# Shifting the start addresses of matmul operands within 512 bytes, stage by stage

## The chip, the cores and the metric

The kernel runs on one NeuronCore of a Trainium2 chip. The metric is the device time of one execution in microseconds, from the first to the last instruction and what lies around them. TensorE (PE) multiplies: each matmul loads a stationary operand of up to 128x128 (LDWEIGHTS, shown as PEld) and then streams a moving operand of up to 512 columns past it; both come from the on-chip memory SBUF, the sum goes to PSUM. VectorE (DVE), ScalarE (ACT) and GpSimd (POOL) work elementwise; transfers are issued from the queues of SyncE (SP), ScalarE and GpSimd.

## The reference

One layer of a streaming encoder on 4096 prompt frames and 32 sample frames, 1024 channels, all in float32:

```python
h = rmsnorm(x, norm_g)
u, v, z_a, xb, z_b = split(h @ w_in)                 # w_in 1024 x 5120
a = u * chunk_mlp(layernorm(v), w_spatial) * silu(z_a)    # 8 heads, 128x128 mixing inside chunks
b = pool_mix(xb) * silu(z_b)                         # trailing means over 2/4/8/16, then 256x256 per group
y = rmsnorm(x + concat(a, b) @ w_out, final_g)       # w_out 2048 x 1024
```

The pooling buffers of both streams and the normalised v rows of the sample frames are outputs as well.

## The kernel before

Each float32 factor is split into a high part (rounded to float32r, the type that TensorE multiplies in one pass) and a low part, and a product of two factors is taken as three matmuls: high x high, high x low, low x high. On top of that each pair of tiles is multiplied by a scheme with 7 products instead of 8 (`NQ = 7`, index `q`), whose operands are sums and differences of quarter blocks. One product `q` is thus 4 slices of the contraction (`k`) times 3 terms, 12 matmuls, all added up in one PSUM bank (lines 188 to 194, `product`); a set of 7 is 84 matmuls of 512 columns.

The work is in stages:

- The first pass (up to about 397 us of the span) normalises and transposes the tokens, makes the operands of all token blocks, and multiplies them with the v columns of `w_in`. Here the moving operand is a weight tile in a `slot` buffer, the stationary one an `op` tile of tokens. 16 pairs of tiles, 16 x 84 = 1344 matmuls.
- Token blocks 0 to 3 (to 1704 us), of 1024 tokens each: 8 gate sets and 8 pool sets per block. The 7 moving operands of a block, one per `q`, stay in the 7 `slot` buffers for the whole block; the stationary operands are weight tiles `wop`, made just ahead by ScalarE (the high part, line 119) and VectorE (the low part, line 81) out of `raw` tiles and of sums of them in `sum` tiles (line 115). Blocks 0 to 2 take 16 x 84 = 1344 matmuls of 512 columns each. Block 3 has the 32 sample frames with it, 528 columns, as 2 x 264: 2688 matmuls. Gate sets also do eight small matmuls for the mixing inside a chunk (line 998). Results pass through `t` tiles and go to DRAM as `abT`.
- The output projection in two halves, `z = 0` and `z = 1` (to the end): the moving operands are weights in the slots again, the stationary ones token tiles in `wop` buffers, read back from `abT`. 16 pairs and 1344 matmuls per half (lines 712 to 714). Sums are made in `y` tiles (line 724).

`product` names the operands: `stationary(s, k)` is 128 floats wide, so it starts at a multiple of 512 bytes within its tile of 1024 floats; `moving(m, k)` starts at a multiple of 512 bytes within the slot in all stages but block 3, where a slice is 528 floats (2112 bytes) long.

The order of the instructions is that in which the code issues them, apart from what the framework's scheduler moves for priority; `prepare` (line 1109 on) makes the stationary operands five products ahead of their use (`LEAD = 5`). When a stage ends, the slot of product `q` is filled anew behind the last product that read it: `Tokens.load` (line 922) and `load_out_weights` (line 632). The last two sets of a stage, and the first two of the next, are interleaved (`lagged`, line 181), so that there are products to do meanwhile. A first filling of the slots for block 0 is in `load_first` (line 589).

SBUF is laid out by pools, each behind the one before; `pool` opens one. The pools `raw_p`, `op_p` (tile `wop`), `sum_p`, and later `t_p`, `cn_p` or `y_p` follow the slots from the left; `WT`, `bias` and the `spare` and `vt` tiles stand at the right end. In the built program the slot buffers begin at byte 18432 (36 x 512) and are 16896 bytes (33 x 512) apart, the first `raw` buffer begins at 136704 (267 x 512), the first `wop` buffer at 161280 (315 x 512), `sum` at 189952 (371 x 512), and `y` and the first `t` at 196096 (383 x 512); `t` tiles are 2176 bytes (4 x 512 + 128), so they follow each other at 0, 128, 256 and 384 past a multiple of 512.

Of the kernel before, what the change touches and what calls it, by code (L numbers as in the profile page):

```python
# [8 lines left out]
F32 = mybir.dt.float32  # L9
F32R = mybir.dt.float32r  # L10
# [5 lines left out]
P = 128  # L16
D = 1024
# [8 lines left out]
NB = 4  # L26
# [3 lines left out]
WIDE = HALF + EXT  # L30
TOT = SEQ + DEC
NQ = 7
WARM = 14


@with_exitstack
def stream_step(ctx: ExitStack, tc, x_prompt, x_sample, state_pool, norm_g, w_in, ln_v_g, ln_v_b,
# [18 lines left out]
    slots = ctx.enter_context(tc.tile_pool(name="slots", bufs=NQ))  # L56
# [45 lines left out]
        return y, guess + 3 * [lambda: stt(t, y, y, m, ALU.mult, ALU.mult),  # L102
                               lambda: stt(y, t, 1.5, y, ALU.add, ALU.mult)]

    def slot():
        return slots.tile([P, 2 * 4 * WIDE], F32R, tag="slot", name="slot")


    behind = []
# [95 lines left out]
    def pool(name, bufs, stack=ctx, **kw):  # L205
        return stack.enter_context(tc.tile_pool(name=name, bufs=bufs, reuse_waits="tile", **kw))
# [4 lines left out]
    with ExitStack() as ph:  # L211
# [23 lines left out]
        def tr_tile():  # L235
            return ps_tr.tile([P, 512], F32, tag="tr", name="tr")

        g_bc = g_p.tile([P, D], F32, name="g_bc")
        first_ops = {}
# [9 lines left out]
        warm = tr_tile()  # L249
        for _ in range(WARM):  # L250
            tc.keep_in_program_order(nc.tensor.transpose(warm[:, :P], ident, ident))
# [10 lines left out]


        wv = [slot()[:, :8 * HALF].rearrange("p (h k n) -> p h k n", h=2, n=HALF) for _ in range(NQ)]

        v_raws = {}
# [87 lines left out]
        class Past:  # L354


            def load(self):
                self.st = half(), half()
                for z in range(2):
                    nc.gpsimd.memset(self.st[z][:HALO], 0.0)  # L360
                    nc.sync.dma_start(self.st[z][1:HALO], state_pool[0, 0, :, z * 512:(z + 1) * 512])
# [226 lines left out]

        def load_first(q):

            first_ops[q] = t = slot()
            dst = t[:, :8 * HALF].rearrange("p (h j x) -> p h j x", h=2, j=4)
            src = xops[0].rearrange("j p (q h x) -> q h p j x", q=NQ, h=2)
            n = 2 if q < NQ - 1 else 4
            for h in range(2):
                nc.sync.dma_start(dst[:, h, :n].bitcast(F32), src[q, h, :, :n])
            if n == 4:
                return
            nc.vector.tensor_copy(dst[:, :, pa.j], pa.ops[q])
            nc.scalar.copy(dst[:, :, pb.j], pb.ops[q])  # L600
# [4 lines left out]
        for n, (pair, q) in enumerate(lagged(pa, pb)):  # L605
            for step in {0: steps[:2], 1: steps[2:3], 2: steps[3:4], 4: steps[4:5], 6: steps[5:6], 7: steps[6:]}.get(n, []):
                step()
            if n == 1:
                norms([], [(v, P) for v in pairs[-3].v])
                pairs[-3].store()  # L610
            pair.product(q)
            if pair is pb:
                load_first(q)


    raw_p = pool("raw_p", 6)
    op_p = pool("wop_p", 7)
    sum_p = pool("sum_p", 3)
    ps_acc = pool("ps_acc2", 6, space=bass.MemoryType.PSUM)
# [10 lines left out]
    w_slots = {}  # L630

    def load_out_weights(z, q):
        w_slots[z, q] = t = slot()[:, :4 * D].rearrange("p (k h n) -> p k h n", k=4, h=2)
        nc.sync.dma_start(t.bitcast(F32), wops[z, q].rearrange("p k (h n) -> p k h n", h=2))

    class OutWeights:
# [227 lines left out]
    with ExitStack() as ph:  # L864
# [50 lines left out]
        class Tokens:  # L915
# [4 lines left out]
                self.groups = [(0, HALF)] if not self.last else [(0, WIDE // 2), (WIDE // 2, WIDE // 2)]  # L920

            def load(self, q):
                t = slot()
                self.ops[q] = t
                if self.last:
                    nc.sync.dma_start(t.bitcast(F32), xops_l[q].rearrange("p x t -> p (x t)"))
                    return
                src = xops[self.b].rearrange("j p (q h x) -> q h p j x", q=NQ, h=2)
                for h in range(2):
                    dst = t[:, h * 4 * HALF:(h + 1) * 4 * HALF].rearrange("p (j x) -> p j x", j=4)  # L930
                    nc.sync.dma_start(dst.bitcast(F32), src[q, h])
# [214 lines left out]
        for n in range(n_sets):  # L1146
# [9 lines left out]
            for s, q in order:  # L1156
                at += 1
                prepare(at + LEAD)
                while later:
                    (later.pop(0) or (lambda: None))()  # L1160
                for c, c0, w in cs[id(s)]:
                    s.product(c, q, c0, w)
                if n == 0 and q == 0:
                    behind.append(s)
                if s is g[-1] and groups[n + 1][0].stage != s.stage:
                    if n + 1 < n_sets:
                        groups[n + 1][0].tok.load(q)
                    else:
                        if q == 3:
                            groups[n_sets][1].begin([raw_tile(), raw_tile()], True)  # L1170
                        load_out_weights(0, q)
                if n == 0 and s is g[-1] and q in (3, 5):
                    next(constants, None)
                if s.kind == "gate" and q in (2, 4):
                    if q == 2:
                        s.t1 = []
                    s.t1.append(s.spatial(len(s.t1)))
                if s.kind == "gate" and q == 6 and s.tok.last:
                    s.spatial_sample()
                if q == NQ - 1:  # L1180
                    later.append(s.finish_gate() if s.kind == "gate" else s.finish_pool())
# [4 lines left out]
    with ExitStack() as ph:  # L1186
# [56 lines left out]
        for n in range(n_sets, len(groups)):  # L1243
# [6 lines left out]
            for m, (s, q) in enumerate(order):  # L1250
                at += 1
                prepare(at + LEAD)
                if m == 0 and n in samples:
                    samples[n].load()
                k = n - n_sets - 4
                if k == KT and m == 2:
                    sample_rows()
                if 0 <= k < KT and m in (0, 2):
                    state_load(k) if m == 0 else state_split()
                s.multiply(q)  # L1260
                if n == n_sets and s is g[0] and q == NQ - 1:
                    s.finish()
                if m == 2 and ended:
                    for x in ended:
                        x.finish()
                if s is g[-1] and n + 1 < len(groups) and groups[n + 1][0].stage != s.stage:
                    load_out_weights(1, q)
                if 0 <= k < KT and m == 6:
                    state_rows(k)
# [34 lines left out]
```

## Time and profile before

| | |
|---|---|
| median of 2 runs | 2346.66 us (2346.46 to 2346.87) |
| profiled execution, span | 2345.9 us |
| TensorE busy | 2328.8 us, 99% |
| weight loads (PEld) busy | 1981.3 us, 84%, beside the matmuls |
| VectorE / ScalarE / GpSimd busy | 1790.2 (76%) / 896.4 (38%) / 215.1 us (9%) |
| granted TensorE clock, mean | 0.999 |
| matmuls of line 193, 512 columns | 4032 with `wop`, 1344 with `op` |
| matmuls of line 193, 264 columns | 2688 |

How to read the lines: a row of a group gives the code line, the engine, the operation, the tiles written and read (out<-in), the count and the mean duration. The duration of a matmul covers its way through the array and overlaps the next one; what counts for the end is the pitch, the time from one start to the next. It is read off the chain of waits, which merges an unbroken run of like matmuls into one piece (start, length, count), or off the starts in a timeline.

### The profile page before, as it was taken

Reading aid. Unit: us, or ns where it says so; the run is one execution under the profiler, and the core shown is the slowest. Engines: PE = TensorE matmul, PEld = TensorE weight load, DVE = VectorE, ACT = ScalarE, POOL = GpSimd, SP = SyncE. Lnnn points to the kernel's source line nnn. Section 1 sums busy time; section 2 is a strip of 40 time slices with the busy share of each in tenths; the row PEclk is TensorE's granted clock in tenths of the full one; section 3 lists DMA queues with packets and bytes.
Section 4 is the critical chain, followed back from the end, with each engine's and each line's share of the span. In section 5 each row is a group of like instructions: output and inputs, shape, how many; then the busy total and the mean of one; then the engine's idle time right before and its main releaser. Section 6 shows DMA issues by size and latency. Waiting matters only on the chain.

```text
span 2345.9 us, 32604 instructions
## 1 busy us (share of the span) xinstructions
PE 2328.8 (99%) x11936; PEld 1981.3 (84%) x11936; DVE 1790.2 (76%) x3318; ACT 896.4 (38%) x1603; POOL 215.1 (9%) x398
## 2 busy tenths in 40 slices
PE   8999999999999999999999999999999999999998
PEld 7878888888888888888888899999987878888877
DVE  7877786866787767877668876668777778688887
ACT  6545544433433333433334333334322333233333
POOL 1010000100021000111000110102200000000000
PEclk9999999999999999999999999999999999999999
DMA  8879977432448334483334472335587776955542
GB/s 309 316 241 279 275 255 245 142 104 89 149 144 296 99 100 134 135 300 122 108 108 148 177 262 87 101 100 164 223 294 265 252 257 232 360 171 169 159 137 90
DMA packets 325145, 445.69 MB, mean 190 GB/s; under 512 B 19324, under 2 KB 248444, under 8 KB 322296
## 3 DMA queue, kind: packets, MB, share of 16 engines
q1 hardware_dynamic: 273384, 355.05, 45.9%
q0 software_dynamic: 22288, 73.48, 8.3%
q10 hardware_dynamic: 29312, 15.08, 2.4%
q8 instruction: 94, 1.54, 0.3%
q14 instruction: 67, 0.55, 0.1%
HBM read 273.88 MB, written 169.66 MB: 189 GB/s over the span
## 4 chain that ended last, share of the span: by engine, by line
PE 95%; DMA 2%; DVE 2%; issue 0%; ACT 0%; SPq 0%; ACTq 0%; DVEq 0%
PE acc L193 66%; PE acc L712 8%; PE acc L713 8%; PE acc L714 8%; PE sp L998 2%; PE tr L473 1%; DMA wops<-raw 1%; DMA vt<-in_w_in_dram 1%; PE acc L261 0%; DMA op<-in_w_in_dram 0%; PE more L844 0%; PE more L843 0%; DVE wop L81 0%; DVE y L724 0%; PE acc L202 0%
## 5 line engine op out<-in xcount | busy, mean ns | idle before, releaser
L193 PE MATMUL acc<-slot,wop 128*128 128x512 f32 (+1 forms) x6720 | 1260.9, 348 | 1.0 <-DVE wop L81 1.0
L193 PEld LDWEIGHTS acc<-slot,wop 128*128 128x128 f32 x6720 | 1081.1, 188 | 156.5 <-DVE wop L81 1.4
L81 DVE TENSOR_TENSOR wop<-raw,wop 128x512 fp32r<-128x512 f32 (+1 forms) x510 | 353.4, 695 | 133.0 <-ACT wop L119 121.7
L119 ACT CAST wop<-raw 128x512 fp32r<-128x512 f32 x340 | 210.5, 622 | 384.4 <-PE acc L193 266.9
L712 PE MATMUL acc<-slot,wop 128*128 128x512 f32 x892 | 347.2, 389 | 1.5 <-DVE y L724 1.5
L713 PE MATMUL acc<-slot,wop 128*128 128x512 f32 x892 | 347.1, 389 | 0.0
L714 PE MATMUL acc<-slot,wop 128*128 128x512 f32 x892 | 347.0, 389 | 0.0
L193 PE MATMUL acc<-slot,op 128*128 128x512 f32 x1344 | 323.8, 395 | 0.3 <-ACT vt L167 0.2
L193 PEld LDWEIGHTS acc<-slot,op 128*128 128x128 f32 x1344 | 247.6, 188 | 51.9 <-ACT vt L167 0.7
L165 DVE TENSOR_TENSOR t<-acc,t 128x512 f32<-128x512 f32 (+1 forms) x320 | 186.7, 584 | 120.0 <-ACT t L174 65.5
L724 DVE TENSOR_TENSOR y<-acc,y 128x512 f32<-128x512 f32 x235 | 159.3, 687 | 72.6 <-PE acc L714 72.2
L712 PEld LDWEIGHTS acc<-slot,wop 128*128 128x128 f32 x892 | 167.4, 188 | 37.8 <-ACT wop L677 2.3
L714 PEld LDWEIGHTS acc<-slot,wop 128*128 128x128 f32 x892 | 167.4, 188 | 34.8
L713 PEld LDWEIGHTS acc<-slot,wop 128*128 128x128 f32 x892 | 167.4, 188 | 34.7
L677 ACT CAST wop<-raw 128x512 fp32r<-128x512 f32 x160 | 98.7, 622 | 175.2 <-PE acc L714 164.9
L81 DVE TENSOR_TENSOR wop<-sum,wop 128x512 fp32r<-128x512 f32 x200 | 136.9, 685 | 25.7 <-ACT wop L119 24.9
L1017 POOL DMA_DIRECT2D abT<-t x128 | 69.2, 541 | 843.2 <-DVE t L1029 622.7
L119 ACT CAST wop<-sum 128x512 fp32r<-128x512 f32 x136 | 84.5, 622 | 96.9 <-PE acc L193 72.0
L1040 DVE TENSOR_TENSOR t<-t 128x527 f32<-128x527 f32 (+3 forms) x160 | 111.1, 698 | 0.6
L677 ACT CAST wop<-sum 128x512 fp32r<-128x512 f32 x64 | 39.7, 622 | 119.5 <-PE acc L714 96.3
L174 ACT COPY t<-acc 128x512 f32<-128x512 f32 (+1 forms) x80 | 40.2, 504 | 107.1 <-PE acc L193 105.4
L115 DVE TENSOR_TENSOR sum<-raw 128x512 f32<-128x512 f32 x68 | 46.8, 688 | 44.7 <-DMA raw<-in_w_in_dram 44.1
(236 smaller groups left out, 1955.0 us busy)
## 6 DMA issues: line engine op xcount, KB each, us to landing
raw<-in_w_in_dram SPq DMA_DIRECT2D x102, 512.0 KB, 4.3
xops<-op SPq DMA_DIRECT2D x72, 512.0 KB, 6.1
abT<-t POOLq DMA_DIRECT2D x128, 256.0 KB, 3.8
raw<-abT SPq DMA_DIRECT2D x64, 512.0 KB, 5.0
slot<-xops SPq DMA_DIRECT2D x30, 1024.0 KB, 9.6
slot<-wops SPq DMA_DIRECT2D x14, 2048.0 KB, 9.7
xt<-in_x_prompt_dram SPq DMA_DIRECT2D x32, 512.0 KB, 5.0
raw<-v_all SPq DMA_DIRECT2D x32, 512.0 KB, 3.3
```

The lines of the kernel that those rows point to most:

```text
L81: return nc.vector.tensor_tensor(out, src, hi.bitcast(F32), ALU.subtract)
L119: pair = nc.scalar.copy(hi, src), lo_part(lo, src, hi)
L165: add = lambda o, x, y: nc.vector.tensor_tensor(o, x, y, ALU.add)
L193: mm(acc, stationary(s, k), moving(m, k), start=fresh and n == 0, stop=n == len(terms) - 1, skip_group_check=True)
L677: nc.scalar.copy(t[:, 0], src)
L712: mm(acc, x[:, 0, k, :], w[:, k, 0, c], start=fresh and k == 0, stop=False, skip_group_check=True)
L713: mm(acc, x[:, 0, k, :], w[:, k, 1, c], start=False, stop=False, skip_group_check=True)
L714: mm(acc, x[:, 1, k, :], w[:, k, 0, c], start=False, stop=k == 3, skip_group_check=True)
L724: nc.vector.tensor_tensor(y, self.acc[bank], y, ALU.add)
L998: mm(sp[:, a, :], self.v[:, 4 * hf + a, :], WT[:, h, :], start=True, stop=True)
L1017: nc.gpsimd.dma_start(abT[row, :, t0:t0 + HALF], t[:, :HALF])
L1040: tt(nxt[:, lo:HALO + m], s[:, lo:HALO + m], s[:, lo - step:HALO + m - step], ALU.add)
```

## The change

Two things are shifted. A pool of one tile of 32 floats (128 bytes) is opened between `raw_p` and `op_p`, so that everything to the left of the gap stays and the `wop`, `sum`, `t` and `y` tiles, and the small tiles behind them, begin 128 bytes further on: `wop` at 161408 in place of 161280. And the slots, which have 128 floats to spare in all stages but block 3, are used from an element given by stage: `SHIFT` has floats for blocks 0 to 3 and for the two halves of the output projection, that is 128, 0, 64, 0, 192 and 256 bytes. The first pass keeps its slots unshifted, and its `op` tiles are not behind the gap.

```diff
+SHIFT = (32, 0, 16, 0, 48, 64)
...
-    def slot():
-        return slots.tile([P, 2 * 4 * WIDE], F32R, tag="slot", name="slot")
+    def slot(shift=0):
+        t = slots.tile([P, 2 * 4 * WIDE], F32R, tag="slot", name="slot")
+        return t[:, shift:] if shift else t
...
-            first_ops[q] = t = slot()
+            first_ops[q] = t = slot(SHIFT[0])
...
     raw_p = pool("raw_p", 6)
+    pool("gap_p", 1).tile([P, 32], F32, name="gap")
     op_p = pool("wop_p", 7)
...
-        w_slots[z, q] = t = slot()[:, :4 * D].rearrange("p (k h n) -> p k h n", k=4, h=2)
+        w_slots[z, q] = t = slot(SHIFT[NB + z])[:, :4 * D].rearrange("p (k h n) -> p k h n", k=4, h=2)
...
-                t = slot()
+                t = slot(SHIFT[self.b])
```

On all five engines the instructions stand in the same order as before; the line numbers of the changed file are one to three higher. One wait sits elsewhere. On VectorE, at the border of the first pass and block 0, before (the tiles: `bn` and `mv` statistics of v rows, `raw` and `sum` the weights of the first sets; the names in brackets are what an instruction waits for, DMAHW0 a DMA queue's semaphore):

```order
L300 BN_STATS bn<-vt 128x6 [waits DVE_49]
L115 TENSOR_TENSOR sum<-raw 128x512 [waits DMASW0_49]
L301 BN_AGGR mv<-bn 128x2 [waits DVE_49]
L115 TENSOR_TENSOR sum<-raw,sum 128x512 [waits DVE_49]
L302 TENSOR_SCALAR na<-mv 128x2 [waits DVE_49]
```

And after:

```order
L302 BN_STATS bn<-vt 128x6 [waits DVE_49]
L117 TENSOR_TENSOR sum<-raw 128x512 [waits DMASW0_49]
L303 BN_AGGR mv<-bn 128x2 [waits DVE_49]
L117 TENSOR_TENSOR sum<-raw,sum 128x512 [waits DMAHW0_49,DVE_49]
L304 TENSOR_SCALAR na<-mv 128x2 [waits DVE_49]
```

The last `sum` buffer now reaches 128 bytes into the place of another `op` tile of the first pass, so its first writer waits for that tile's store; before, only the first `t` tile lay there, and its first writer, 37 rows further down, waited.

## The prediction

> **What bounds the kernel now.** I read the page first, then the chain of waits, then the starts and durations of the matmuls themselves.
>
> ```profile
> span 2345.9 us, 32604 instructions
> ...
> PE 2328.8 (99%) x11936; PEld 1981.3 (84%) x11936; DVE 1790.2 (76%) x3318; ACT 896.4 (38%) x1603; POOL 215.1 (9%) x398
> ...
> PEclk9999999999999999999999999999999999999999
> ...
> PE 95%; DMA 2%; DVE 2%; issue 0%; ACT 0%; SPq 0%; ACTq 0%; DVEq 0%
> PE acc L193 66%; PE acc L712 8%; PE acc L713 8%; PE acc L714 8%; PE sp L998 2%; PE tr L473 1%; DMA wops<-raw 1%; DMA vt<-in_w_in_dram 1%; PE acc L261 0%; DMA op<-in_w_in_dram 0%; PE more L844 0%; PE more L843 0%; DVE wop L81 0%; DVE y L724 0%; PE acc L202 0%
> ```
>
> TensorE is busy for 2328.8 of 2345.9 us at an undiminished clock, and 90% of the chain that ends last is four lines of matmuls, all of the type that reads a stationary tile (`wop` or `op`) and a moving tile (`slot`). Nothing else sets the end. So the change can only act in two ways: by altering the time from one such matmul to the next (the pitch, below), or by making TensorE wait for something that does not hold it up today.
>
> The pitch comes out of the chain, which merges unbroken runs, and of TensorE's timeline near the end:
>
> ```profile
> 601.11 165.98 PE acc L193 x732
> ...
> 920.30 165.99 PE acc L193 x732
> ...
> 1581.58 122.82 PE acc L193 x1008
> ```
>
> ```profile
> 2333.75 0.39 PE L712 MATMUL acc<-slot,wop 128*128 128x512 f32 x1
> ...
> 2335.11 0.28 PE L712 MATMUL more<-slot,wop 128*128 128x256 f32 x1
> 2335.22 0.28 PE L713 MATMUL more<-slot,wop 128*128 128x256 f32 x1
> ...
> 2337.86 0.28 PE L714 MATMUL more<-slot,wop 128*128 128x256 f32 x1
> ```
>
> A run of 732 matmuls of 512 columns takes 165.98 us, a pitch of 226.75 ns (the first such run is 504 matmuls of token block 0 and 228 of block 1, the second the same of blocks 1 and 2); the output projection has the same (six from 2333.75 to 2335.11, 226.7 ns). The matmuls of 256 columns run 22 pitches from 2335.22 to 2337.86: 120.0 ns. So a column costs (226.75 - 120.0) / 256 = 0.417 ns and each matmul 120.0 - 106.75 = 13.25 ns on top, whatever its width. That 13.25 ns is what a shift of addresses could touch: over the 512-column matmuls it is 6% of the pitch.
>
> By the sizes in the code (`wop` tiles of 4096 bytes, `slot` tiles of 33 x 512 bytes) all these operands begin at a multiple of 512 bytes today, with one exception: token block 3. There a moving row is 528 floats, 2112 bytes, so its starts fall on 64k + 256h + 32c bytes (k from 0 to 3, h and c 0 or 1): all sixteen multiples of 32 below 512, each against a stationary operand at 0. At 0.417 ns per column plus 13.25 ns its 264 columns would have a pitch of 123.3 ns; the row of 1008 above gives 122.82 / 1008 = 121.85 ns. A block with every offset is thus 1.5 ns per matmul better than one with none, on the mean. The spread is in the durations:
>
> ```profile
> L193 PE MATMUL acc<-slot,wop x825: 278/284/388, 1599.7 to 1700.0; 128*128 128x264 f32 x165
> ...
> L193 PE MATMUL acc<-slot,wop x663: 387/389/412, 609.8 to 759.9; 128*128 128x512 f32 x166
> ...
> L712 PE MATMUL acc<-slot,wop x45: 389/389/389, 2099.9 to 2129.8; 128*128 128x512 f32 x45
> ```
>
> (least, median, longest in ns; one line per stretch: block 3, block 1, output.) Where all offsets are alike, the least and the median are 2 ns apart or nothing; in block 3 the best is 6 ns below the median. Offset may matter, then, for single matmuls, but a width of 264 could do the same, since it is no multiple of the 256 above.
>
> **The change part by part.** *The matmuls.* No instruction is added, removed or moved, so what each matmul does stays, and only the start addresses differ. The offset of moving against stationary operand becomes: first pass (v projection, `op` with `slot`) 0 as before; block 0 128 - 128 = 0; block 1 0 - 128 = -128; block 2 64 - 128 = -64; output half 0 192 - 128 = +64; half 1 256 - 128 = +128. Block 3 keeps the set of sixteen offsets, in another order, since subtracting 128 from all multiples of 32 modulo 512 gives them again: 0 by that argument. If the offset counts, four stages of 16 x 84 = 1344 matmuls can move, 5376 in all. Their price is seen in no row directly. Bounds: at best the fixed 13.25 ns goes altogether, 5376 x 13.25 = 71 us less; the best single matmuls of block 3 are 6 ns under the median, 32 us less; the mean of block 3 is 1.5 ns better, 8 us less. At worst the regular spacing is lost. That is to be seen where stationary operands of changing width alternate in the output stage:
>
> ```profile
> 1761.37 0.39 PE L843 MATMUL more<-slot,wop 128*64 128x512 f32 x1
> ...
> 1764.82 0.40 PE L845 MATMUL more<-slot,wop 128*64 128x512 f32 x1
> ```
>
> Between these two lie 15 pitches, 3.45 us, 230.0 ns: 3.3 ns above the regular 226.7, or 18 us over 5376. The durations there give a farther end: their median in the row below is 397 ns, 8 ns above the 389 of the regular ones, or 43 us.
>
> ```profile
> L844 PE MATMUL more<-slot,wop x32: 388/397/399, 1761.6 to 2242.1; 128*32 128x512 f32 x32
> ```
>
> I take 0. The pitch is the same to a fraction of a nanosecond in block 0, block 1 and the output stage, while DMA, VectorE and ScalarE do quite different things beside them. Such a value looks like a cost of the matmul's own sequence, not of a collision in memory. The nearest row with other offsets, block 3, is only 1.5 ns off on the mean and has another width.
>
> The Trainium skill, "SBUF — State Buffer", section "Who interferes with whom", gives TensorE two independent read ports, one for the moving operand and one for the weights, and says it never waits on anyone; by that rule the four stages change by 0 us. The 278 to 288 ns within block 3 are not explained by it, so the trace agrees only for the stages with like offsets. "TensorE: Matmul & The Clock Gate", section "Wait — 56ns, not 53.3ns?", has a warm matmul of 512 columns at 215.7 ns, so 11 of the 13.25 ns would be avoidable; by it the best case would be an estimate of 59 us rather than 71.
>
> *Sums, results and weights.* `wop`, `sum`, `y` and the `t` tiles move by 128 bytes, which VectorE and ScalarE write and read.
>
> ```profile
> L81 DVE TENSOR_TENSOR wop<-raw,wop 128x512 fp32r<-128x512 f32 (+1 forms) x510 | 353.4, 695 | 133.0 <-ACT wop L119 121.7
> ...
> L1029 DVE TENSOR_TENSOR t<-t 128x512 f32<-128x512 f32 x48 | 33.2, 691 | 1.0
> ```
>
> A `t` tile is 544 floats, 2176 bytes, so the ten of them already stand at 0, 128, 256 and 384 past a multiple of 512, and their sums take 691 ns, like the 695 of `wop` and `raw`, which all stand at 0. Cost 0. Even 10 ns on each of the 3318 VectorE instructions would be 33 us on an engine that is idle for 24% of the span and works five products ahead of TensorE.
>
> *The loads into slots.* They write 64 to 256 bytes further on.
>
> ```profile
> slot<-xops SPq DMA_DIRECT2D x30, 1024.0 KB, 9.6
> ...
> DMA to landing us min/median/max: 3.8/9.5/17.9
> ```
>
> A slot is refilled behind the last product that reads it, and the interleaved order of two sets leaves at least nine products, 9 x 12 x 226.75 ns = 24.5 us, until it is read. The slowest landing is 17.9 us; without that cover each late load would hold TensorE for the difference. A load would have to become 6.6 us slower than the slowest to show. Cost 0.
>
> *One wait.* The gap makes the last `sum` buffer overlap one more `op` tile of the first pass, so VectorE's L115 waits for the store of that tile, which a later instruction waited for before. Queued behind it on VectorE are the low parts of block 0's first weights, for which TensorE would wait.
>
> ```profile
> 371.91 0.33 SPq L485 DMA_DIRECT2D xops<-op  x1
> ...
> 399.80 0.69 DVE L115 TENSOR_TENSOR sum<-raw,sum 128x512 f32<-128x512 f32 x1
> ...
> xops<-op SPq DMA_DIRECT2D x72, 512.0 KB, 6.1
> ```
>
> The store is issued at 371.91 and lands about 6 us later, 22 us before the wait. Cost 0.
>
> The sum is 2345.9 us of span and no change. The median of the runs, 2346.66, lies 0.8 us above the span of the profiled execution: forecast **2346.5 us**.
>
> **The rivals.** *The offset opens a faster spacing* in some stages. For it speaks block 3's spread; against it that block's mean, since fifteen of its sixteen offsets are not 0 and most of the 13.25 ns is still paid. Its time is 8 to 32 us less: 2338 to 2314. *All offsets but 0 are free of a collision:* 59 to 71 us less, 2275 to 2288; the same mean speaks hard against it. *The regular spacing is lost:* equal starts may be what lets the matmuls settle into 226.75 ns, and an offset of 64 or 128 bytes leaves them in the unsettled state that the mixed widths show at 230.0. Place: blocks 1 and 2 and both output halves; price 3.3 ns each, 18 us, so 2364; with the 8 ns of the durations 43 us, 2389. It decides as soon as one stage of 1344 averages over 227.5 ns (1 us a stage). For it speaks that the spacing does react to the width of the neighbouring operand; against it that it holds over runs of 732 across the border of two blocks. That the change does not do what it says is excluded by the built addresses: `wop` moves from 161280 to 161408.
>
> **How the numbers follow.** No change 0.58; faster spacing 0.20; all of it free 0.06; spacing lost 0.16, a quarter of that near its far end. The range goes from the end of the second case, 2312, to a little past the price of the lost spacing, 2368; left out are the free case (0.06) and the upper part of the slow one (0.07). A difference of over 2% is 47 us. Faster than 2300: the free case and a sliver of the second, 0.08. Slower than 2393, more than the far end: 0.04. Within: 0.88.
>
> **What would show it.** Runs of 732 in blocks 0, 1 and 2 again at 165.98 us, output rows again at 226.7 ns and 389 ns, block 3's run of 1008 at 122.8 +- 1 us, VectorE's L81 and L1029 within 3 ns. I am wrong if block 1 or 2 departs from block 0 in its run, or one output half from the other: then the offset counts, and the sign and size per stage say how.

## The result and the profile after

The changed kernel takes 2376.48 us (2376.41 to 2376.55) against 2346.66 us: a ratio of 1.0125, with a 95% interval of 1.0095 to 1.0154. It is 30 us slower, and the span of its profiled execution grows from 2345.9 to 2374.6 us, by 28.7 us.

The page of the changed kernel (its lines are one to three numbers higher than before: L193 is L195, L712 to L714 are L715 to L717):

```profile
span 2374.6 us, 32604 instructions
...
PE 2359.2 (99%) x11936; PEld 1984.3 (84%) x11936; DVE 1795.3 (76%) x3318; ACT 896.7 (38%) x1603; POOL 212.4 (9%) x398
...
PEclk9999999999999999999999999999999999999999
...
L82 DVE TENSOR_TENSOR wop<-raw,wop 128x512 fp32r<-128x512 f32 (+1 forms) x510 | 353.3, 695 | 145.4 <-ACT wop L121 133.8
...
L715 PE MATMUL acc<-slot,wop 128*128 128x512 f32 x892 | 351.7, 394 | 1.4 <-DVE y L727 1.4
...
L195 PE MATMUL acc<-slot,op 128*128 128x512 f32 x1344 | 323.8, 395 | 0.3 <-ACT vt L169 0.2
```

Two of these groups in the page of before:

```profile
L712 PE MATMUL acc<-slot,wop 128*128 128x512 f32 x892 | 347.2, 389 | 1.5 <-DVE y L724 1.5
...
L193 PE MATMUL acc<-slot,op 128*128 128x512 f32 x1344 | 323.8, 395 | 0.3 <-ACT vt L167 0.2
```

TensorE is as full as before at the same clock, and busy for 30 us more. VectorE's low parts in `wop` still take 695 ns, so the shifted writes cost nothing. The first pass, whose operands did not move, has the same 323.8 us and 395 ns. The matmuls themselves are further apart. TensorE's waits have not grown: the 1.4 us before L715 were 1.5 before.

The two runs of 732 that the prediction named, 165.98 and 165.99 us before, are now these:

```profile
600.92 167.26 PE acc L195 x732
924.70 170.30 PE acc L195 x732
```

The first has 504 matmuls of block 0 and 228 of block 1 and gains 1.3 us, the second 504 of block 1 and 228 of block 2 and gains 4.3 us. Block 1 departs from block 0, which was the sign of being wrong.

Stage by stage this is seen in the same chain of waits. In a gate set the small matmuls of line 998 break the run, and the 60 matmuls between two such breaks are merged into one piece. Of before (start in us, length, count), one piece each of blocks 0, 1 and 2:

```profile
455.14 13.62 PE acc L193 x60
...
795.18 13.62 PE acc L193 x60
...
1114.38 13.62 PE acc L193 x60
```

Of the changed kernel, the same places:

```profile
454.39 13.65 PE acc L195 x60
...
796.86 13.94 PE acc L195 x60
...
1123.77 14.00 PE acc L195 x60
```

Block 0, where moving and stationary operand start 128 bytes past a multiple of 512 together, is nearly where it was: 0.5 ns per matmul in these pieces, and nothing in the pitch below. Block 1 (distance -128 bytes) pays (13.94 - 13.62) / 60 = 5.3 ns, block 2 (-64) 6.3 ns. In the output half 1, a window of 120 us holds fewer matmuls. A row has the window, its length, and then the busy time and count of TensorE, the weight loads, VectorE, ScalarE and GpSimd; the row of before, then that of after:

```profile
2060.00:2180.00 120.00, 120.00 (x531) 99.37 (x530) 105.61 (x228) 46.64 (x98) 7.44 (x14) 1.00 0.56 180
```

```profile
2060.00:2180.00 120.00, 120.00 (x518) 97.30 (x517) 98.73 (x207) 44.07 (x92) 6.38 (x12) 1.00 0.54 175
```

531 / 518 times 226.7 ns gives 232.4 ns. The settled pitch below is the mean time from one start to the next over all matmuls that are at least 24 behind a break (some 850 to 1300 in a stage). It is 226.7 ns in block 0, 232.5 in block 1, 233.3 in block 2, 229.9 in output half 0 and 232.4 in half 1. Times 1344, the differences to before are 7.8 + 8.9 + 4.3 + 7.7 = 28.7 us. Blocks 0 and 3 add 0.6 and 0.8 us, and block 0 starts 0.8 us earlier, so the stages make up the difference of the spans within about 1 us.

### The profile page after: what moved, and what is told of

Same layout as the page of the kernel before. It is cut to its first block, busy times and chain, and to the rows that moved or that the text cites. A ratio compares the mean times of both kernels' runs of the same rounds, so it can differ in the third digit from the quotient of the medians.

```text
span 2374.6 us, 32604 instructions
## 1 busy us (share of the span) xinstructions
PE 2359.2 (99%) x11936; PEld 1984.3 (84%) x11936; DVE 1795.3 (76%) x3318; ACT 896.7 (38%) x1603; POOL 212.4 (9%) x398
## 4 chain that ended last, share of the span: by engine, by line
PE 89%; issue 6%; DMA 3%; DVE 2%; POOL 0%; ACT 0%; SPq 0%; POOLq 0%; ACTq 0%; DVEq 0%
PE acc L195 65%; PE acc L715 6%; PE acc L717 6%; PE acc L716 6%; PE sp L1001 2%; PE tr L475 1%; DMA vt<-in_w_in_dram 1%; DMA wops<-raw 1%; DMA op<-in_w_in_dram 0%; POOL part L738 0%; DMA part<-y 0%; DVE wop L82 0%; PE acc L204 0%; PE more L847 0%; PE acc L203 0%
## 5 line engine op out<-in xcount | busy, mean ns | idle before, releaser
L195 PE MATMUL acc<-slot,wop 128*128 128x512 f32 (+1 forms) x6720 | 1278.5, 350 | 1.0 <-DVE wop L82 1.0
L195 PEld LDWEIGHTS acc<-slot,wop 128*128 128x128 f32 x6720 | 1082.0, 188 | 172.6 <-DVE wop L82 1.4
L715 PE MATMUL acc<-slot,wop 128*128 128x512 f32 x892 | 351.7, 394 | 1.4 <-DVE y L727 1.4
L717 PE MATMUL acc<-slot,wop 128*128 128x512 f32 x892 | 351.4, 394 | 0.0
L716 PE MATMUL acc<-slot,wop 128*128 128x512 f32 x892 | 350.1, 393 | 0.0
L195 PE MATMUL acc<-slot,op 128*128 128x512 f32 x1344 | 323.8, 395 | 0.3 <-ACT vt L169 0.2
L195 PEld LDWEIGHTS acc<-slot,op 128*128 128x128 f32 x1344 | 247.6, 188 | 51.9 <-ACT vt L169 0.7
L715 PEld LDWEIGHTS acc<-slot,wop 128*128 128x128 f32 x892 | 167.9, 188 | 40.4 <-ACT wop L680 2.1
L717 PEld LDWEIGHTS acc<-slot,wop 128*128 128x128 f32 x892 | 167.9, 188 | 38.8
L167 DVE TENSOR_TENSOR vt<-acc,vt 128x512 f32<-128x512 f32 x64 | 44.1, 688 | 42.6 <-ACT vt L176 29.2
```

Source lines behind the costliest of these rows:

```text
L167: add = lambda o, x, y: nc.vector.tensor_tensor(o, x, y, ALU.add)
L195: mm(acc, stationary(s, k), moving(m, k), start=fresh and n == 0, stop=n == len(terms) - 1, skip_group_check=True)
L715: mm(acc, x[:, 0, k, :], w[:, k, 0, c], start=fresh and k == 0, stop=False, skip_group_check=True)
L716: mm(acc, x[:, 0, k, :], w[:, k, 1, c], start=False, stop=False, skip_group_check=True)
L717: mm(acc, x[:, 1, k, :], w[:, k, 0, c], start=False, stop=k == 3, skip_group_check=True)
```

## The experiments

**Is it the distance of the two operands, or the shift itself?** All five slot shifts were set to the 128 bytes of the gap:

```diff
-SHIFT = (32, 0, 16, 0, 48, 64)
+SHIFT = (32, 32, 32, 0, 32, 32)
```

> The gap stays and the slots are shifted by the same 128 bytes in blocks 0, 1, 2 and both output halves, so that moving and stationary operands start at equal offsets again, 128 past a multiple of 512. Theory A, the distance between the two starts sets the pitch: the pitch is 226.7 ns in all five stages, block 3 stays at its 122.7 ns of the changed kernel, and the time is 2346 to 2348 us. Rival B, the shifted sums and results or the absolute place of the stationary operand cost the 30 us: the time stays near 2376 us, at least 2365. Rival C, each stage pays for its absolute slot offset: 128 bytes in five stages costs at least what the second output half paid for 256, some 8 us, so 2355 or more.

Measured: 2350.65 us, ratio 1.0011 (1.0002 to 1.0021). The settled pitch is 226.7 to 226.8 ns in all five stages; the chain shows 166.0 us again for its runs of 732:

```profile
601.02 166.02 PE acc L195 x732
920.86 166.02 PE acc L195 x732
```

Theory A holds in the pitch, B and C fall. A's time, 2346 to 2348 us, was nearly 3 us too low. What stays is not in the settled pitch. The profiled execution, the longest of the ten, has a span of 2352.5 us against 2345.9: blocks 0 to 2 are 0.6 us longer each and block 3 is 0.8, but most of it, 4.5 us, is in output half 0. There TensorE waits 4.0 us instead of 1.5 for the `y` sums, and shortly after the longest of these waits the granted clock is 0.50 from 1940.3 to 1943.6 us, with 427 ns from one matmul to the next.

```profile
PE acc L715 <- DVE y L727: 4.0, 3, 2.0
```

**Do the sums and results matter by themselves?** The gap was moved behind the weight tiles and no slot was shifted:

```diff
-SHIFT = (32, 0, 16, 0, 48, 64)
+SHIFT = (0, 0, 0, 0, 0, 0)
...
     raw_p = pool("raw_p", 6)
+    op_p = pool("wop_p", 7)
     pool("gap_p", 1).tile([P, 32], F32, name="gap")
-    op_p = pool("wop_p", 7)
```

> No slot is shifted, and the gap stands behind the weight tiles, so only sum, t and y tiles move by 128 bytes; stationary and moving operands stand as before. Theory A: 2346 to 2347 us. Rival B, sums and results cost the time: some part of the 30 us, 2355 us or more, with VectorE's groups on those tiles longer by 10 ns or more.

Measured: 2347.91 us (one run; 2347.45 for the kernel before), 226.7 ns in all five stages, and VectorE's groups on the moved `y`, `sum` and `t` tiles within 1 ns of the 687, 689 and 691 ns of before:

```profile
L727 DVE TENSOR_TENSOR y<-acc,y 128x512 f32<-128x512 f32 x235 | 159.2, 686 | 72.9 <-PE acc L717 72.4
...
L117 DVE TENSOR_TENSOR sum<-raw,sum 128x512 f32<-128x512 f32 x68 | 46.8, 688 | 1.3
...
L1032 DVE TENSOR_TENSOR t<-t 128x512 f32<-128x512 f32 x48 | 33.2, 691 | 1.0
```

The shifted sums and results cost nothing that can be seen.

**What does each distance cost?** Without the gap, the slots alone were shifted, in each run by another amount in each of the five stages:

```diff
-SHIFT = (32, 0, 16, 0, 48, 64)
+SHIFT = (8, 24, 40, 0, 48, 56)
...
-    pool("gap_p", 1).tile([P, 32], F32, name="gap")
```

> No gap; slots shifted by 32 (block 0), 96 (block 1), 160 (block 2), 192 (output half 0) and 224 bytes (half 1), stationary at 0. Theory A gives each stage a pitch of its own between 224 and 236 ns, constant within the stage in the pool sets, and no stage has to be above 226.7. A collision that any distance but 0 avoids would give 216 ns; a cost that any distance but 0 brings (the lost spacing of the prediction) gives 229 ns or more in all five, 2365 us or more.

The second and third scan differ from the first in the shifts alone:

```diff
+SHIFT = (64, 72, 80, 0, 88, 104)
```

> No gap; slots shifted by 256 (block 0), 288 (block 1), 320 (block 2), 352 (half 0) and 416 bytes (half 1). Theory A: again a pitch per distance; if the pattern repeats after 256 bytes, 256 gives 226.7 ns. If every distance but 0 costs: 229 ns or more in all five, 2365 us or more. From block 3 of before, where the starts at 256 had the shortest durations, block 0 should be the best stage, below 226.7 ns.

```diff
+SHIFT = (4, 2, 1, 0, 60, 63)
```

> No gap; slots shifted by 16 (block 0), 8 (block 1), 4 (block 2), 240 (output half 0) and 252 bytes (half 1), stationary at 0. The runs so far gave 226.7 ns at a distance of 0 and of 256 bytes and 229.9 to 235 ns at every other multiple of 32. If the distance counts in units of 64 bytes or more with a best point at 0, 4 to 16 bytes cost 0 to 3 ns and the time is 2347 to 2362 us. If only exact equality settles the spacing, all five stages stand at 230 ns or more, 2365 us or more. If 0 is a peak between two lower values, one of the five lies below 226 ns.

Measured: 2390.78, 2376.91 and 2403.24 us, one run each, against 2347.45 (for the first two) and 2348.76 us of the kernel before. From the second, the gate-set pieces of blocks 0, 1 and 2 (shifts of 256, 288 and 320 bytes), and those of the third (16, 8 and 4 bytes):

```profile
454.25 13.62 PE acc L195 x60
...
796.29 14.00 PE acc L195 x60
...
1101.80 13.75 PE acc L195 x60
```

```profile
455.85 13.90 PE acc L195 x60
...
783.36 14.41 PE acc L195 x60
...
1120.31 14.39 PE acc L195 x60
```

256 bytes is as good as 0 (13.62), so the pattern repeats after 256 bytes; in the table below 32 and 288, 96 and 352, 160 and 416 agree as well. Eight bytes are the worst, 14.41 us for 60 or 240 ns each. All settled pitches of this study, by the distance of moving start minus stationary start modulo 256 bytes, worked out from the starts as above:

| distance, bytes | pitch, ns | in |
|---|---|---|
| 0 | 226.7 to 226.8 | every stage of before and of the equal shifts; block 0 at 256 |
| 4, 8 | 240.0, 240.0 | blocks 2 and 1 of the fine scan |
| 16 | 231.7 | block 0 of the fine scan |
| 32 | 233.3, 233.3 | block 0 of scan a, block 1 (288) of scan b |
| 64 | 229.9, 228.9 | half 0 of the change, block 2 (320) of scan b |
| 96 | 233.3, 233.3 | block 1 of scan a, half 0 (352) of scan b |
| 128 | 232.5, 232.4 | block 1 and half 1 of the change |
| 160 | 234.3, 234.3 | block 2 of scan a, half 1 (416) of scan b |
| 192 | 233.3, 233.3 | block 2 of the change, half 0 of scan a |
| 224 | 233.3 | half 1 of scan a |
| 240, 252 | 234.6, 231.1 | halves 0 and 1 of the fine scan |

Equal distances agree to 0.2 ns, at 64 bytes to 1 ns, whichever stage they stand in and whichever of the two operands was shifted. So the claim that single offsets open a faster spacing falls: of twelve distances other than 0, none is below 226.7 ns, and block 0 of the second scan, expected below that, is level with it. That the distance counts in units of 64 bytes falls too: 4 and 8 bytes cost 13.3 ns and not 0 to 3. "Only exact equality settles the spacing" was right in size, but not in its words. Some of the others are just as constant, only longer: of the 1327 times from one start to the next in block 2, 1308 are 233 or 234 ns in the changed kernel, and 1294 are 240 ns at 4 bytes. In scan a, by contrast, the matmuls take turns between 230 and 238 ns about a steady mean.

**Is it the amount read for the weights?** In the changed kernel, the stationary operands were cut to 64 of 128 columns, save where a fresh bank has to be filled; half of each product is left out:

```diff
-            mm(acc, stationary(s, k), moving(m, k), start=fresh and n == 0, stop=n == len(terms) - 1,
+            r = P if fresh and n == 0 else rows
+            mm(acc[:r], stationary(s, k)[:, :r], moving(m, k), start=fresh and n == 0, stop=n == len(terms) - 1,
```

(with `rows` 64 for the sets, and the same in the output's product)

> The changed kernel (distances 0, -128, -64, block 3, +64, +128) with the stationary operand of every product of blocks and output cut to 64 of its 128 columns, save the first matmul of a fresh bank; half of each product is left out. Theory D, the time above the columns' own comes from reading the weights beside the moving operand, byte for byte: with half the bytes the excess over 213 ns about halves in every stage, 220 ns in block 0 and 221 to 224 in the others, about 2300 us. Rival E, it is where the two streams stand to each other that counts and not how long the weight load reads: the pitches stay within 2 ns of the changed kernel's 226.7, 231, 233.3, 229.9 and 231, and the time at 2365 to 2380 us.

Measured: 2364.94 us, one run. The weight loads do become shorter, with a median of 135 ns in place of 188 (the two rows are TensorE's matmuls and weight loads in a stretch of block 2), and the pitch hardly follows:

```profile
L196 PE MATMUL acc<-slot,wop x516: 388/396/483, 1109.7 to 1240.0; 128*64 128x512 f32 x172
L196 PEld LDWEIGHTS acc<-slot,wop x515: 133/135/192, 1109.9 to 1240.0; 128*64 128x64 f32 x172
```

The pitches are 229.6 (block 1), 232.0 (block 2), 228.3 and 229.4 ns (output): 1.4 to 2.9 ns less than with full weights. Theory D asked for half of the excess over the columns' own time. By the prediction's line that time is 226.75 - 13.25 = 213.5 ns, so the half would be 8 to 10 ns. At distance 0, in block 0, the pitch rises from 226.7 to 229.9 ns. Theory D falls. E is right that the amount isn't what counts, but not within its 2 ns everywhere, and the time lies just below its 2365 us. The regular spacing of distance 0 needs the regular width as well. Widths that alternate are not the reason: only 64 of block 0's 1344 matmuls are at full width here, and far from them the same six pitches return over and over (230, 236, 229, 224, 227 and 234 ns).

**Does the absolute place count?** Gap and slots shifted together, by 64 and by 32 bytes:

```diff
-    pool("gap_p", 1).tile([P, 32], F32, name="gap")
+    pool("gap_p", 1).tile([P, 16], F32, name="gap")
-SHIFT = (32, 0, 16, 0, 48, 64)
+SHIFT = (16, 16, 16, 0, 16, 16)
```

> Gap and all slot shifts are 64 bytes: distance 0 in blocks 0 to 2 and both output halves, and block 3 with its sixteen distances in another order. If only the distance counts, and not how far past a multiple of 256 both stand, the five stages are at 226.7 ns and the time within 4 us of before; block 3, whose mean was 122.3 ns per start-to-start before and 122.65 behind a gap of 128, stays within 1 ns, 3 us either way. If the absolute place counts too: 229 ns or more in the five stages, 2360 us or more.

> The same with 32 bytes. If only the distance counts: 226.7 ns in the five stages, within 4 us of before, block 3 within 1 ns of 122.3. If the absolute place counts: the 233 ns that a slot shift of 32 bytes alone gave in block 0, 2380 us or more.

Measured: 2348.93 us, ratio 1.0006 (0.9997 to 1.0016), and 2350.27 us, 1.0011 (1.0001 to 1.0020). All five stages are at 226.7 to 226.8 ns in both. A slot shift of 32 bytes alone gave 233.3 ns; with the stationary operand shifted along the pitch is back at 226.7. In these five stages only the distance counts, at multiples of 32 bytes; whether both could stand 4 or 8 bytes off together was not tried. The 2.7 us that stay at 32 bytes lie elsewhere: in that run's profile block 3 is 2.1 us longer than before, 0.8 ns per matmul, and output half 0 is 2.7 us longer, with another stretch at a clock of 0.50 (1936.9 to 1940.2 us). Why block 3, whose set of distances is the same, gets longer is not shown.

No experiment gave a version faster than the kernel before.

## Why the prediction was wrong

- **What bounds the kernel** was right: matmul after matmul on TensorE, no wait that grew, and the change acts through the pitch alone. The list of the distances by stage was right too, and with it which stages would move.
- **The step that failed is "I take 0"** for the four stages with a new distance. The size in its place is 3.2 to 6.6 ns per matmul, 28.7 us in sum. Two arguments led there. The first was that a pitch that is the same beside quite different work looks like the matmul's own sequence and not like a matter of memory. But at other distances it is just as constant, in block 2 at 233.3: constancy told that nothing else disturbs it, not that addresses are without effect.
- The second was **block 3 as the nearest row**. Its 264 columns were held against a line through 256 and 512 columns at distance 0, and came out 1.5 ns better. The narrow matmuls at the end of half 1 show why that can't be carried over. In the changed kernel, at distance 128, 22 pitches lie between these two starts:

```profile
2363.93 0.29 PE L716 MATMUL more<-slot,wop 128*128 128x256 f32 x1
...
2366.55 0.28 PE L717 MATMUL more<-slot,wop 128*128 128x256 f32 x1
```

  That is 2.62 us, 119.1 ns each, where distance 0 had 120.0. The same matmuls of the scans, at the end of their half 1, have 118.7 ns at 224 bytes, 117.4 at 160 and 116.7 at 252, and every run with equal starts has 120.0 again. So with 256 columns each of these four distances is better than 0, and with 512 columns each is worse, by 4.4 to 7.6 ns. Block 3's 264 columns, better than the line, fit the narrow case and said nothing on 512 columns. A "cost per matmul whatever its width" was a line through two widths at distance 0, and holds at no other distance measured. Block 3 itself did what was forecast (its set of distances is the same): under 1 us.
- **The lost spacing**, the rival on the slow side, is what happened, in its four stages and by its price's sign. Its near price, 3.3 ns from matmuls of mixed width, was too small, and its far price, 8 ns, too large; the measured mean of 5.3 ns lies between. Its picture of an unsettled spacing fits in part: in block 1 the matmuls do vary (228 to 241 ns), and in both halves, but in block 2 the spacing is settled and only longer. The range stopped just past the near price and should have reached to the middle of the two; it left a case out whose price had been written down. (The two chances left out, 0.06 and 0.07, leave 0.87 and not 0.88; nothing hangs on it.)
- **The two faster rivals** fall: no stage of 512 columns settled below 226.7 ns in any run.
- **The rule on ports** of the Trainium skill ("SBUF — State Buffer", "Who interferes with whom"), that TensorE never waits on anyone and that its two reads are independent, would have given 0 us. The runs differ: two operands of TensorE itself, 8 bytes apart in place of 0, make a matmul 13.3 ns longer. How the two reads come to affect each other is not shown.
- **Sums, results, loads and the moved wait** cost nothing, as forecast: VectorE's 695 ns are unchanged, and TensorE waits for no slot.

What remains open is the mechanism. Shown is that the distance of the starts modulo 256 bytes sets the pitch of the 512-column stages, that both operands count there only relative to each other, and that the width of the weights and of the moving operand changes the pattern. A guess that two reads meet in the same part of the memory would fit a period of 256 bytes, but equal starts are then the best and not the worst, and half the weights do not take half the excess away; no run here shows what happens inside.

## What to carry to other kernels

Where float32r matmuls of 512 columns run back to back as they do here, let moving and stationary operands start at the same place modulo 256 bytes: at every other distance tried the pitch was 1 to 6% longer. At 256 columns it was the other way round, so measure the width that you have. A pitch that is constant to a nanosecond isn't for that reason the hardware's best; only a run with another layout tells. A row for another width is no bound, and does not even give the sign.

## What the runs showed of the hardware that was not expected

- The sharpness: 4 or 8 bytes of distance cost 13.3 ns, more than any larger one, while 252 bytes (4 less than the period) cost 4.4 ns. It is not symmetrical.
- The agreement: the same distance gives the same pitch to 0.2 ns in most cases, in a block, where a moving row is four runs of 512 bytes 2048 apart, and in the output stage, where it is 2048 bytes in one piece.
- Narrow matmuls prefer the opposite: 256 columns have 120.0 ns at distance 0, the longest of the five distances measured, and 119.1, 118.7, 117.4 and 116.7 at 128, 224, 160 and 252.
